# Where the softmax division, the weight loads and a rotary product stand in a hybrid attention layer

## The chip, the cores and the metric

The kernel runs on one core of a Trainium2 chip. Its engines are PE (matrix products), DVE (elementwise and reductions), ACT (activations and copies with a scale), POOL (elementwise, SBUF only) and SP, whose queue issues every DMA of this kernel. The time is device microseconds of one launch, the median of several. All arithmetic is done at about float32 precision: a float32 product is made of three matmuls of split operands (hi x hi, hi x lo, lo x hi), and a probability is carried as two float16 numbers, hi and lo, whose sum it is.

## What is computed

One encoder layer on x (1024 tokens, 1024 features). adaLN gives shift, scale and gate from a conditioning vector. The mixer projects the normalised x and has two groups of heads: 8 heads of multi-head latent attention (MLA; chunk-causal, dense, head size 96 of which 32 are rotary) and 8 heads of chunked attention over a band of 9 chunks of 64 keys with a relative bias (CA; head size 64). Cut to what matters here:

```python
q = jnp.dot(rmsnorm(q_lat, g_q_latent[l]), w_q_up[l]).reshape(B, S, MLA_HEADS, MLA_QK)
kv = jnp.dot(rmsnorm(kv_lat, g_kv_latent[l]), w_kv_up[l]).reshape(B, S, MLA_HEADS, MLA_NOPE + MLA_V)
k_nope, v = kv[..., :MLA_NOPE], kv[..., MLA_NOPE:]
k = jnp.concatenate([k_nope, jnp.broadcast_to(k_rope[:, :, None, :], ...)], axis=-1)
q = rmsnorm(q, g_mla_q[l])
k = rmsnorm(k, g_mla_k[l])
q = jnp.concatenate([q[..., :MLA_NOPE], rope(q[..., MLA_NOPE:], positions)], axis=-1)
k = jnp.concatenate([k[..., :MLA_NOPE], rope(k[..., MLA_NOPE:], positions)], axis=-1)
o_mla = mla_attention(q, k, v)        # softmax(q k^T * scale, masked) v, per head
...
o_ca = chunk_attention(cq, ck, cv, rel_bias[l])
mixed = jnp.dot(jnp.concatenate([o_mla, o_ca], axis=-1), w_out[l])
x = x + g_a[:, None, :] * mixed
h = modulate(rmsnorm(x, g_mlp_norm[l]), sh_m, sc_m)
u = causal_dwconv(jnp.dot(h, w_up[l]), conv_w[l], conv_b[l])
gate, val = jnp.split(u, 2, axis=-1)
x = x + g_m[:, None, :] * jnp.dot(jax.nn.silu(gate) * val, w_down[l])
```

## The kernel before

Tokens come in 8 tiles of 128. The attention is cut into 32 units, a unit being one head and one half (four tiles) of its queries: 16 CA units, then 16 MLA units (lines 814 to 816). A loop over all 128 query tiles (817 to 828) calls `scores` of one tile and `values` of the tile three before. Between them `pace` draws steps from a list of fillers, generators that make the projections: v and q, k of the CA heads, then `m` (the latents), `up0` and `up1` (`f_up`, the up-projections of four MLA heads each) and `oca` (`f_oca`, the CA half of the output projection, kept in DRAM as `part_d`). So the fillers' matmuls run beside the attention of earlier heads. The order of the instructions on each engine is fixed when the kernel is built, by a planner that plays the program through with estimated times and with priorities (`high_priority`); on the chip each engine works its queue in that order and waits at semaphores.

A query tile (`scores`, 636 to 707): PE makes the negated scores into one of two PSUM buffers `S`. DVE adds bias or mask and takes the row minimum m. ACT makes P = exp(m - s) into one of three P buffers, with the row sum. DVE makes the reciprocal of the sum and multiplies it by 2^15 (lines 685, 686). POOL makes hi = float16(P x reciprocal) (`scale_pool`, line 71), DVE makes lo = P x reciprocal - hi (703), both into one of three `hl` buffers, and a DMA transpose on SP's queue (705) brings hi and lo into one of three `PT` buffers. Tiles of more than 640 keys go in two pieces. `values` (709 to 726) multiplies them by v into a PSUM bank; at the end of a unit ACT (723) and DVE (724) take the two halves of v's own split out of it, undo the scales, and a DMA writes the result to `oT_d` in DRAM.

An up-projection (`f_up`, 517 to 582) loads w_q_up's two blocks and w_kv_up's block (526, 532) through `qtile`, a ring of two buffers, splits them (ACT hi, POOL lo), and for each token tile makes q (384 columns) and k, v (512). For q: squares on ACT, their sums on DVE, the reciprocal root on POOL (`rsqrt_mean`, 113 to 116: one instruction scales and adds epsilon, one raises to the power -1/2), the product with it on DVE (561), the rotary turn of 32 of 96 columns on POOL (`rope_apply`, 461 to 470). For k the same, with the rotary part's sum of squares added on POOL (578) and the rotary part, turned earlier in `f_m`, multiplied by the root on POOL (582).

`f_oca` (598 to 611) loads its weights (`load_wo`, 586 to 596, through the same ring) and, for each of 2 x 8 steps, the transposed CA outputs `cl`, splits them, multiplies and stores. After the attention the other half of w_out is loaded (836) and the output projection of the MLA heads runs (873 to 894): `ol` loads the MLA outputs, `pa` the kept part, x1 the residual. Then the MLP's pages, its 22 up-projection steps and the down-projection follow; the change touches nothing there.

Of the kernel before, what the change touches and what calls it, by code (L numbers as in the profile page):

```python
# [41 lines left out]
MODE_C = "1111"  # L42
MODE_M = "1111"
PSCALE, VSCALE = 2.0 ** 15, 2.0 ** 14
# [18 lines left out]
def layer_kernel(ctx, tc, I, out):  # L63
# [273 lines left out]
    def pow2_scale(nm, ssw, b2, n, fac):  # L337
# [13 lines left out]
        dve.tensor_scalar(ab[:, 1:2], t[:, 2, 1:2], 1.0 / (VSCALE * PSCALE), None, op0=MUL)  # L351
# [109 lines left out]
    def rope_apply(o, x, tab, t, nh, tmp):  # L461
# [5 lines left out]
        pool.tensor_tensor(a, x, ct, op=MUL)  # L467
        pool.tensor_tensor(b, x, sn, op=MUL)
        pool.tensor_tensor(o[:, :, 0:16], a[:, :, 0:16], b[:, :, 16:32], op=SUB)
        pool.tensor_tensor(o[:, :, 16:32], a[:, :, 16:32], b[:, :, 0:16], op=ADD)  # L470

    def f_m():
        w = load_w("wm_", I["w_m"], NM)
        lat = {}
        for t in range(NT):
# [17 lines left out]
            lat[t] = raw  # L493
            if j == 3:
# [21 lines left out]

    def f_up(gr):
        if gr == 0:
            right.__exit__(None, None, None)
            for i in "4v3":  # L520
                G["cm" + i] = tc.tile_pool(name="gp" + i, bufs=1, side="right", reuse_waits="tile")
                G[i] = G["cm" + i].__enter__()
        wq = []
        for k in range(2):
            raw = qtile(f"wqr{gr}_{k}")
            sp.dma_start(raw[:, :384], I["w_qu"][gr][:, k, :])
            w = g4([P, 2, 512], F32R, f"wq{gr}_{k}")
            hi_of("a", w[:, 0, :384], raw[:, :384])
            lo_of("p", w[:, 1, :384], raw[:, :384], w[:, 0, :384])
            wq.append(w)  # L530
        raw = qtile(f"wkr{gr}")
        sp.dma_start(raw[:], I["w_kvu"][gr])
# [9 lines left out]
        for t in range(NT):  # L542
            h, j = divmod(t, 4)
            sl = slice(j * P, (j + 1) * P)
            if t % 2 == 0:
# [6 lines left out]
            raw = rtile(f"uqr{gr}_{t}")  # L552
            act.activation(raw[:, :384], pt[:, :384], AF.Copy)
            sq = qtile(f"usq{gr}_{t}")
            act.activation(sq[:, :384], raw[:, :384], AF.Square)
            ss = cst.tile([P, 4], F32, name=f"uss{gr}_{t}", tag="ss", bufs=4)
            r = cst.tile([P, 4], F32, name=f"ur{gr}_{t}", tag="rr", bufs=4)
            dve.tensor_reduce(ss[:], sq[:, :384].rearrange("p (a b) -> p a b", a=4), axis=AX.X, op=ADD)
            rsqrt_mean(r[:], ss[:], QK)
            q_t = mq[gr, t // 2][:, t % 2]  # L560
            dve.tensor_tensor(q_t, raw[:, :384].rearrange("p (a b) -> p a b", a=4),
                              r[:].unsqueeze(2).to_broadcast([P, 4, QK]), op=MUL)
            rope_apply(q_t[:, :, NOPE:], q_t[:, :, NOPE:], tabq, t, 4, raw[:, 0:256])
# [5 lines left out]
            act.activation(r3, p4[:, :, 0:NOPE], AF.Copy)  # L569
            v_t = mv[gr, t // 2][:, t % 2]  # L570
            act.activation(v_t[:, :, 0, :], p4[:, :, NOPE:], AF.Copy, scale=sc)
            dve.scalar_tensor_tensor(v_t[:, :, 1, :], p4[:, :, NOPE:], sc, v_t[:, :, 0, :], op0=MUL, op1=SUB)
            s3 = raw[:, 256:512].rearrange("p (a b) -> p a b", a=4)
            act.activation(s3, r3, AF.Square)
            ss = cst.tile([P, 4], F32, name=f"kss{gr}_{t}", tag="ss", bufs=4)
            r = cst.tile([P, 4], F32, name=f"kr{gr}_{t}", tag="rr", bufs=4)
            dve.tensor_reduce(ss[:], s3, axis=AX.X, op=ADD)
            pool.tensor_tensor(ss[:], ss[:], ssr[:, t:t + 1].to_broadcast([P, 4]), op=ADD)
            rsqrt_mean(r[:], ss[:], QK)
            k_t = mk[gr, t // 2][:, t % 2]  # L580
            dve.tensor_tensor(k_t[:, :, 0:NOPE], r3, r[:].unsqueeze(2).to_broadcast([P, 4, NOPE]), op=MUL)
            pool.tensor_tensor(k_t[:, :, NOPE:], kr[:, t:t + 1, :].to_broadcast([P, 4, ROPE]),
                               r[:].unsqueeze(2).to_broadcast([P, 4, ROPE]), op=MUL)


    def load_wo(k0, n, he, le):
        ws = []
        for k in range(k0, k0 + 4):
            raw = qtile(f"wor{k}_{n}")
            sl = slice(n * 512, (n + 1) * 512)  # L590
            sp.dma_start(raw[:], I["w_out"][k * P:(k + 1) * P, sl])
            w = g4([P, 2, 512], F32R, f"wo{k}_{n}")
# [5 lines left out]
    def f_oca():  # L598
        for n in range(2):
            ws = load_wo(4, n, "a", "p")  # L600
            for t in range(NT):
                lo = rtile(f"cl{t}_{n}", (P, 4, P), F32R)
                hi = rtile(f"ch{t}_{n}", (P, 4, P), F32R)
                sp.dma_start(f32(lo[:]), oT_d[4:8, :, t * P:(t + 1) * P].rearrange("k p t -> p k t"))
                hi_of("a", hi[:], f32(lo[:]))
                lo_of("p", lo[:], f32(lo[:]), hi[:])
                pt = ps.tile([P, 512], F32, name=f"oc{t}_{n}", tag="mm", bufs=2)
                yield from gemm3_f(pt[:], [(hi[:, k], lo[:, k], ws[k][:, 0], ws[k][:, 1]) for k in range(4)])
                o = qtile(f"co{t}_{n}")
                act.activation(o[:], pt[:], AF.Copy)  # L610
# [541 lines left out]
```

## Time and profile before

| | us |
|---|---|
| median of 3 runs | 1465.47 (1463.65 to 1468.99) |
| the profiled execution | 1464.36 |
| its span | 1462.2 |

Busy time over the whole span, and the share of it:

| engine | busy us | share |
|---|---|---|
| PE | 1278.0 | 87% |
| PE's weight loads | 1058.7 | 72% |
| DVE | 1013.6 | 69% |
| ACT | 611.4 | 42% |
| POOL | 823.0 | 56% |

The shares are means over stages with different limits. The stages can be told apart by which instructions run: the start with adaLN and the first projections to about 105 us, the CA units to about 400, the two up-projections to about 510, most of the MLA units to about 660, the output projection and the MLP's first pages to about 780, the up-projection of the MLP to about 1190, the down-projection to the end. A page of the profile gives the span in 40 equal slices; the line of POOL in it, busy tenths, and that of the granted clock of PE, in tenths of full speed:

```profile
POOL 5263554274599954534644555566655555665662
PEclk9979987999787899996887999999999999999998
```

Slices 12 to 14 of POOL (402 to 512 us) stand at 9, 9 and 9, the up-projections. The chain of waits that ended last, followed back through the whole execution, has 39% of the span on PE, 17% on DMA, 15% on DVE, 13% on POOL and 12% in which the engine waited for nothing that the profile shows.

### The profile page before, as it was taken

What the parts mean: (1) busy time and instruction counts of PE and PEld (TensorE: products, weight loads), DVE (VectorE), ACT (ScalarE), POOL (GpSimd) and SP (SyncE); (2) the same over time, 40 slices, a digit from 0 to 9 for tenths busy, and PEclk for the clock granted to TensorE, in tenths of its full rate; (3) what the DMA queues carried; (4) which work ended last, traced back from release to release, by engine and by line L of the source; (5) the groups of instructions that cost most, each with busy time, mean ns of one, the idle gap of its engine ahead of it and who ended that gap; (6) DMA issues with size and microseconds to landing.
All of it is one profiled execution on the core that took longest, in us unless ns stands there. A gap on an engine that the chain in (4) does not pass through costs nothing.

```text
span 1462.2 us, 20198 instructions
## 1 busy us (share of the span) xinstructions
PE 1278.0 (87%) x6836; PEld 1058.7 (72%) x6836; DVE 1013.6 (69%) x1734; ACT 611.4 (42%) x1190; POOL 823.0 (56%) x845
## 2 busy tenths in 40 slices
PE   3859989998967788885776999999999998999997
PEld 2759878886756666664655878788888887887885
DVE  6874776476667868872476887777777777566653
ACT  4453354243455545543274434344444433332331
POOL 5263554274599954534644555566655555665662
PEclk9979987999787899996887999999999999999998
DMA  7323647455522577879611322322222244446442
GB/s 281 134 71 74 131 114 148 129 119 120 112 52 51 115 163 156 180 142 253 246 72 59 105 110 101 116 87 87 87 87 83 75 140 164 151 144 238 146 142 101
DMA packets 218595, 185.94 MB, mean 127 GB/s; under 512 B 148086, under 2 KB 183034, under 8 KB 217468
## 3 DMA queue, kind: packets, MB, share of 16 engines
q1 hardware_dynamic: 218492, 184.66, 44.5%
q8 instruction: 54, 0.88, 0.3%
q14 instruction: 49, 0.40, 0.1%
HBM read 121.17 MB, written 28.84 MB: 103 GB/s over the span
## 4 chain that ended last, share of the span: by engine, by line
PE 39%; DMA 17%; DVE 15%; POOL 13%; issue 12%; ACT 3%; SPq 1%; DVEq 0%; POOLq 0%; ACTq 0%
POOL wds L82 5%; DMA aw<-w_ada 5%; PE p L924 4%; PE p L926 4%; PE p L925 4%; DMA wu<-w_up 3%; DMA PTm<-hlm 3%; PE sc L658 2%; PE dnp L1067 2%; PE dnp L1069 2%; PE dnp L1068 2%; PE sm L658 2%; DVE adacc L243 2%; DVE aacc L430 1%; DVE u L1002 1%
## 5 line engine op out<-in xcount | busy, mean ns | idle before, releaser
L82 POOL TENSOR_TENSOR wds<-wd,wds 128x512 fp32r<-128x512 f32 x88 | 154.6, 1777 | 99.0 <-ACT wds L75 99.0
L82 POOL TENSOR_TENSOR wc<-ws,wc 128x512 fp32r<-128x512 f32 x22 | 65.4, 2972 | 137.8 <-ACT wc L75 137.8
L1057 DVE TENSOR_TENSOR wd<-wd,gmbc 128x1024 f32<-128x1024 f32 x44 | 67.5, 1533 | 80.4 <-DMA wd<-w_down 80.4
L1069 PE MATMUL dnp<-wds,g 128*128 128x512 f32 x308 | 118.4, 390 | 4.5 <-DVE g L82 4.5
L1067 PE MATMUL dnp<-wds,g 128*128 128x512 f32 x308 | 119.6, 390 | 1.9 <-DVE xo L1075 1.9
L75 ACT ACTIVATE wds<-wd 128x512 fp32r<-128x512 f32 x88 | 54.8, 624 | 157.3 <-PE dnp L1069 152.2
L1068 PE MATMUL dnp<-wds,g 128*128 128x512 f32 x308 | 119.5, 389 | 0.0
L71 POOL TENSOR_SCALAR hlm<-Pm,rim 128x512 f16<-128x512 f32 (+4 forms) x88 | 61.9, 706 | 70.1 <-DMA PTm<-hlm 55.1
L703 DVE SCALAR_TENSOR_TENSOR hlm<-Pm,rim,hlm 128x512 f16<-128x512 f32 (+4 forms) x88 | 68.0, 777 | 30.1 <-POOL hlm L71 29.7
L71 POOL TENSOR_SCALAR hlc<-Pc,ric 128x640 f16<-128x640 f32 (+2 forms) x64 | 45.3, 710 | 76.9 <-DVE ric L686 41.2
L1015 DVE TENSOR_TENSOR ws<-wu,wu 128x512 f32<-128x512 f32 x22 | 30.7, 1396 | 76.2 <-DMA wu<-w_up 76.2
L82 DVE TENSOR_TENSOR g<-gr,g 128x512 fp32r<-128x512 f32 x44 | 71.9, 1635 | 11.5 <-ACT g L75 11.5
L1001 DVE SCALAR_TENSOR_TENSOR u<-c,pk,u 128x1023 f32<-128x1023 f32 x44 | 77.4, 1765 | 2.0 <-ACT u L1000 2.0
L1036 ACT ACTIVATE u<-u 128x1024 f32<-128x1024 f32 x22 | 23.4, 1063 | 132.1 <-DVE u L1002 132.1
L683 ACT ACTIVATE Pc<-sc,mc 128x640 f32<-128x640 f32 (+2 forms) x64 | 42.1, 659 | 82.5 <-DVE mc L673 62.0
L658 PE MATMUL sm<-mk,mq 96*128 96x512 f32 (+3 forms) x288 | 68.9, 372 | 7.9 <-ACT Pm L683 7.3
L1000 ACT ACTIVATE u<-c,pk 128x1024 f32<-128x1024 f32 x44 | 52.3, 1236 | 56.2 <-DVE c L1032 56.2
L716 PE MATMUL pvm<-PTm,vt 128*128 128x128 f16 x576 | 50.5, 242 | 28.8 <-DMA PTm<-hlm 24.3
L658 PE MATMUL sc<-k,q 64*128 64x512 f32 (+3 forms) x288 | 70.3, 372 | 4.9 <-ACT Pc L683 3.0
L430 DVE SCALAR_TENSOR_TENSOR aacc<-aw,cs,aacc 128x256 f32<-128x256 f32 x84 | 44.9, 535 | 40.6 <-DMA aw<-w_ada 40.0
L716 PEld LDWEIGHTS <-vt 128*128 128x128 f16 x576 | 41.1, 109 | 41.7 <-issue 38.3
L1069 PEld LDWEIGHTS dnp<-wds,g 128*128 128x128 f32 x308 | 57.8, 188 | 17.7 <-DVE g L82 5.7
(368 smaller groups left out, 4342.0 us busy)
## 6 DMA issues: line engine op xcount, KB each, us to landing
wu<-w_up SPq DMA_DIRECT2D x44, 512.0 KB, 4.3
wd<-w_down SPq DMA_DIRECT2D x44, 512.0 KB, 4.7
aw<-w_ada SPq DMA_DIRECT2D x96, 128.0 KB, 2.3
g_d<-u SPq DMA_DIRECT2D x22, 512.0 KB, 2.6
gr<-g_d SPq DMA_DIRECT2D x44, 256.0 KB, 3.7
x<-x SPq DMA_DIRECT2D x16, 512.0 KB, 8.3
adaw<-w_ada_a SPq DMA_DIRECT2D x8, 1024.0 KB, 5.5
wq_r<-w_qk SPq DMA_DIRECT2D x32, 128.0 KB, 2.6
```

The costliest lines, as they stand in the source:

```text
L71: pool.tensor_scalar(o, i, s, 1.0, op0=MUL, op1=MUL)
L82: (pool if eng == "p" else dve).tensor_tensor(o, i, f32(hi), op=SUB)
L430: dve.scalar_tensor_tensor(acc[:], w[:], cs[:, k:k + 1], acc[:], op0=MUL, op1=ADD)
L658: last = pe.matmul(s[:, c:c + w], qpg[rs_, a, q], kpgs[kh][rs_, b, ko:ko + w], start=(a == 0 and b == 0), stop=(a == 1))
L703: dve.scalar_tensor_tensor(hl[:, w:2 * w], pp, ri[:], hl[:, :w], op0=MUL, op1=SUB)
L716: last = pe.matmul(u.pv[:, c], u.vst(j), mov, start=(x == 0), stop=(x == len(todo) - 1))
L924: pe.matmul(pt, sh, pg[:, 0], start=(k == 0), stop=False)
L1001: dve.scalar_tensor_tensor(u[:, 1:], c[:, :S - 1], pk[:, cv + 1:cv + 2], u[:, 1:], op0=MUL, op1=ADD)
L1057: dve.tensor_tensor(raw[:], raw[:], gmbc[:], op=MUL)
L1067: pe.matmul(pts[t][n], sh, w[n][:, 0], start=(j == 0), stop=False)
L1068: pe.matmul(pts[t][n], sh, w[n][:, 1], start=False, stop=False)
L1069: pe.matmul(pts[t][n], sl, w[n][:, 0], start=False, stop=(j == NF - 1))
```

## The change

Three edits, made together.

1. The exponentials are split undivided. The factor 2^15 goes into the exponent: log(2^15) is added to m on DVE before the exponential. hi is a plain copy of P to float16 on ACT and lo = P - hi on DVE, without a scalar. The sums of a unit's four tiles are kept in one tile; at the end of the unit DVE takes their reciprocals, PE multiplies each, broadcast to 128 columns, by the identity, which lays the reciprocal of every query along the columns of a PSUM bank in all rows, and DVE multiplies the output by it.
2. Loads go one step ahead. `fetch_up` issues the three loads of an up-projection early (for the first at token tile 4 of `f_m`, for the second at token tile 3 of the first); `fetch_wo` does so for blocks of w_out, `split_wo` splits them later, and the MLA half of w_out is loaded and partly split inside `f_oca`. The raw weights stand in the six buffers that the CA heads' v tiles use (`v16`). `f_oca` loads the next step's `cl` before it multiplies the present one.
3. In the up-projection q and k of a token tile share one reciprocal root of eight columns, taken after k's squares are there. The addition of the rotary part's squares (578) and the rotary part's product (582) go from POOL to DVE. `rope_apply` gets an argument for its engine, which stays POOL.

```diff
-PSCALE, VSCALE = 2.0 ** 15, 2.0 ** 14
+LOGP, VSCALE = 15 * math.log(2.0), 2.0 ** 14
...
+            if t == 4:
+                fetch_up(0)
...
+    def vtile(name):
+        return apg.tile([P, 512], F32, name=name, tag="v16", bufs=6)
+
+    def fetch_up(gr):
+        r = up_raw[gr] = [vtile(f"wqr{gr}_{k}") for k in range(3)]
+        for k in range(2):
+            sp.dma_start(r[k][:, :384], I["w_qu"][gr][:, k, :])
+        sp.dma_start(r[2][:], I["w_kvu"][gr])
...
+            if t == 3 and gr == 0:
+                fetch_up(1)
+            if t == 5 and gr == 1:
+                fetch_wo(4, 0)
...
+            ss = cst.tile([P, 8], F32, name=f"uss{gr}_{t}", tag="ss", bufs=4)
+            r = cst.tile([P, 8], F32, name=f"ur{gr}_{t}", tag="rr", bufs=4)
...
-            rsqrt_mean(r[:], ss[:], QK)
-            q_t = mq[gr, t // 2][:, t % 2]
...
+            dve.tensor_reduce(ss[:, 4:8], s3, axis=AX.X, op=ADD)
+            dve.tensor_tensor(ss[:, 4:8], ss[:, 4:8], ssr[:, t:t + 1].to_broadcast([P, 4]), op=ADD)
+            rsqrt_mean(r[:], ss[:], QK)
...
-            pool.tensor_tensor(ss[:], ss[:], ssr[:, t:t + 1].to_broadcast([P, 4]), op=ADD)
-            rsqrt_mean(r[:], ss[:], QK)
...
-            pool.tensor_tensor(k_t[:, :, NOPE:], kr[:, t:t + 1, :].to_broadcast([P, 4, ROPE]),
-                               r[:].unsqueeze(2).to_broadcast([P, 4, ROPE]), op=MUL)
+            dve.tensor_tensor(k_t[:, :, NOPE:], kr[:, t:t + 1, :].to_broadcast([P, 4, ROPE]),
+                              r[:, 4:8].unsqueeze(2).to_broadcast([P, 4, ROPE]), op=MUL)
...
+    def fetch_wo(k0, n):
+        r = wo_raw[k0, n] = [vtile(f"wor{k}_{n}") for k in range(k0, k0 + 4)]
+        for i in range(4):
+            sp.dma_start(r[i][:], I["w_out"][(k0 + i) * P:(k0 + i + 1) * P, n * 512:(n + 1) * 512])
...
     def f_oca():
...
+        lo = fetch(0)
+        for s in range(2 * NT):
+            n, t = divmod(s, NT)
+            hi = rtile(f"ch{t}_{n}", (P, 4, P), F32R)
+            hi_of("a", hi[:], f32(lo[:]))
+            lo_of("p", lo[:], f32(lo[:]), hi[:])
+            nxt = fetch(s + 1) if s + 1 < 2 * NT else None
+            if t == 2:
+                fetch_wo(4 * (1 - n), 1 - n)
...
+            if t == 5:
+                ws.append(split_wo(4 * (1 - n), 1 - n, "a", "p"))
+            lo = nxt
+        fetch_wo(0, 1)
+        wo.append(ws[2])
...
-                act.activation(pr[:, :n], sv, AF.Exp, bias=m[:], scale=-1.0, accum_out=rsum[:, 0:1])
+                dve.tensor_scalar(m[:], m[:], LOGP, None, op0=ADD)
+                act.activation(pr[:, :n], sv, AF.Exp, bias=m[:], scale=-1.0, accum_out=u.rsum[:, i % 4:i % 4 + 1])
             with tc.high_priority(offset=OFF_P):
-                dve.reciprocal(ri[:], rsum[:, 0:1])
-                dve.tensor_scalar(ri[:], ri[:], PSCALE, None, op0=MUL)
...
-                        if mode == "1":
-                            scale_pool(hl[:, :w], pp, ri[:])
...
-                        dve.scalar_tensor_tensor(hl[:, w:2 * w], pp, ri[:], hl[:, :w], op0=MUL, op1=SUB)
+                    act.activation(hl[:, :w], pp, AF.Copy)
+                    dve.tensor_tensor(hl[:, w:2 * w], pp, hl[:, :w], op=SUB)
...
+                    ri = cst.tile([P, 4], F32, name=f"ri{u.nm}_{u.g}", tag="ri", bufs=2)
+                    dve.reciprocal(ri[:], u.rsum[:])
+                    rb = ps.tile([P, 512], F32, name=f"rb{u.nm}_{u.g}", tag="T", bufs=TB)
+                    for j in range(4):
+                        pe.matmul(rb[:, j * P:(j + 1) * P], ri[:, j:j + 1].to_broadcast([P, P]), ident[:],
+                                  start=True, stop=True)
                     act.activation(sb[r0], u.pv[r1], AF.Copy, scale=inv[r1])
                     dve.scalar_tensor_tensor(dst[r0], u.pv[r0], inv[r0], sb[r0], op0=MUL, op1=ADD)
+                    dve.tensor_tensor(dst[r0], dst[r0], rb[r0], op=MUL)
...
-    wo = [load_wo(0, n, "a", "v" if n else "p") for n in range(2)]
+    wo.append(split_wo(0, 1, "a", "v"))
```

More of the change, by code (lines that the diff above doesn't have):

```diff
@@ L598, in f_oca, with fetch @@
     def f_oca():
[L599 to L610, printed above, removed]
-                sp.dma_start(part_d[t][:, n * 512:(n + 1) * 512], o[:])
+        ws = [split_wo(4, 0, "a", "p")]
+        def fetch(s):
+            lo = rtile(f"cl{s}", (P, 4, P), F32R)
+            t = s % NT
+            sp.dma_start(f32(lo[:]), oT_d[4:8, :, t * P:(t + 1) * P].rearrange("k p t -> p k t"))
+            return lo
+        lo = fetch(0)
[7 more added lines that the diff above has]
+                fetch_wo(4 * (1 - n), 1 - n)
+            pt = ps.tile([P, 512], F32, name=f"oc{t}_{n}", tag="mm", bufs=2)
+            yield from gemm3_f(pt[:], [(hi[:, k], lo[:, k], ws[n][k][:, 0], ws[n][k][:, 1]) for k in range(4)])
+            o = qtile(f"co{t}_{n}")
+            act.activation(o[:], pt[:], AF.Copy)
+            sp.dma_start(part_d[t][:, n * 512:(n + 1) * 512], o[:])
+            if t == 5:
[3 more added lines that the diff above has]
+        wo.append(ws[2])
+    wo, wo_raw, up_raw = [], {}, {}
     def qk_page(src, name, rows, tag, bufs, gain):
```

73 lines of the change are left out of this document (26 added, 47 removed).

## The prediction

> **What bounds the kernel now.** I read the busy time by stage first, because the change touches only 105 to 780 us of the span; the 680 us behind that (the gated MLP) and the first 105 us keep their instructions. Columns: PE, PEld, DVE, ACT, POOL busy, granted clock, DMA share, GB/s.
>
> ```profile
> 105.00:200.00 95.00, 94.11 (x751) 85.32 (x749) 59.45 (x176) 38.40 (x90) 41.11 (x53) 1.00 0.45 101
> 200.00:300.00 100.00, 94.36 (x658) 82.60 (x657) 64.44 (x194) 41.09 (x106) 43.11 (x54) 0.85 0.57 130
> 300.00:400.00 100.00, 88.01 (x547) 75.05 (x547) 67.44 (x195) 43.50 (x133) 59.66 (x110) 0.91 0.55 120
> 400.00:440.00 40.00, 26.57 (x122) 20.51 (x122) 28.21 (x79) 21.04 (x55) 37.55 (x74) 0.84 0.26 60
> 440.00:510.00 70.00, 53.69 (x307) 43.48 (x307) 56.05 (x142) 39.41 (x92) 66.88 (x117) 0.81 0.39 81
> 510.00:660.00 150.00, 127.31 (x878) 101.69 (x877) 113.58 (x272) 75.38 (x155) 72.56 (x86) 0.95 0.76 160
> 660.00:780.00 120.00, 74.81 (x342) 58.54 (x341) 66.05 (x82) 50.11 (x85) 54.81 (x49) 0.76 0.54 172
> ```
>
> There are four stages with four limits. The band attention (105 to 400) is bound by PE: its projection matmuls follow one another with some 12 us of gaps after 200. The two up-projections (400 to 510) are bound by POOL (37.55 of 40, 66.88 of 70). The latent attention (510 to 660) has no full engine. What limits it shows in POOL's longest wait of that window (total, times, longest):
>
> ```profile
> POOL hlm L71 <- DMA PTm<-hlm: 50.6, 30, 4.3
> ```
>
> and in the instructions of a probability tile (by shape, whole span: busy, mean ns, idle before):
>
> ```profile
> L703 DVE SCALAR_TENSOR_TENSOR hlm<-Pm,rim,hlm 128x512 f16<-128x512 f32 x40 | 34.1, 853 | 17.3 <-POOL hlm L71 17.2
> ...
> L71 POOL TENSOR_SCALAR hlm<-Pm,rim 128x512 f16<-128x512 f32 x40 | 30.4, 759 | 39.4 <-DMA PTm<-hlm 30.3 <-DVE rim L686 4.2 <-DVE sm L676 2.4
> ...
> L622 DVE TENSOR_TENSOR mq<-mq_ps,mq 96x512 fp32r<-96x512 f32 x16 | 10.8, 677 | 0.1
> ...
> L685 DVE RECIPROCAL rim<-rsm 128x1 f32<-128x1 f32 x64 | 9.7, 153 | 6.2 <-ACT Pm L683 5.8
> ```
>
> POOL stands 50.6 us because the three hl buffers come free only when the DMA transposes of older tiles have landed. The turn of one buffer is hi (0.76), lo (0.85), the landing (3.3, median of the DMA issues) and what each queues for; 64 pieces in 150 us, three at a time, make a turn of 7.0 us. The last stage (660 to 780) begins with weights that come late.
>
> **The rows of the change.** POOL's work in the up-projections (by shape, 400 to 510), and two places where a load is late (ACT's timeline; in brackets the idle time before):
>
> ```profile
> L116 POOL TENSOR_TENSOR kr<-kss,nhalf 128x4 f32<-128x4 f32 x16 | 16.5, 1029 | 0.5
> L116 POOL TENSOR_TENSOR ur<-uss,nhalf 128x4 f32<-128x4 f32 x16 | 16.2, 1010 | 0.2
> ...
> L582 POOL TENSOR_TENSOR kn<-kr,kr 128x128 f32<-128x128 f32 x15 | 8.4, 557 | 0.6
> ...
> L578 POOL TENSOR_TENSOR kss<-kss,ssr 128x4 f32<-128x4 f32 x16 | 4.4, 278 | 0.1
> ```
>
> ```profile
> 444.33 0.42 ACT L535 ACTIVATE wkj<-wkr 128x256 f32<-128x256 f32 x1 [4.94 <-DMA wkr<-w_kvu]
> ...
> 676.34 0.63 ACT L75 ACTIVATE wo<-wor 128x512 fp32r<-128x512 f32 x1 [8.86 <-DMA wor<-w_out]
> ```
>
> **Reciprocals by matmul: a loss in the band stage.** Each of 32 units (16 band, 16 latent) gains four matmuls of 128 columns with an f32 row of reciprocals broadcast as weights. The nearest row is the gate's broadcast, L456: four calls of 256 columns are recorded as 8 matmuls of 377 ns, those of 512 columns take 590, so a call is two passes and a pass costs 213 ns per 256 columns. Four calls of 128 columns are 8 passes of 0.107, 0.86 us, with the change of operands some 0.95 per unit. From below, the transposes of L618 (one pass, four in 0.60 us) give 0.45; from above, 8 weight loads of 0.19 (L456) in the open give 1.5. I take 0.95, because operands and types are those of L456. In the band stage PE has no room: 16 x 0.95 = +15 us (7 to 24). POOL and DVE work that goes there shortens only the 12 or so us that PE stands idle between 200 and 400: -3. Sum +12. In the latent stage 16 x 0.95 falls into 23 us of idle PE, mostly.
>
> **Up-projections: gain.** POOL now does per tile two rsqrts of four columns (1.03 + 1.01, and 0.24 + 0.23 for their scaling), the sum of squares' addition (0.28) and the rotary part (0.56). The eight-column rsqrt is there in the band's norms (L116, 1.65 us; L115, 0.2 to 0.4). So 1.3 to 1.4 us of some 4.6 leave per tile. With the scaling of P (0.7 us, 2 to 4 pieces before 440, 15 after) POOL falls from 37.5 to some 25 in the first window and from 66.9 to 45 in the second. DVE takes up 0.3 for the rotary part (L411, a 128x256 form, is 0.48) and 0.15 for the addition: 8 x 0.45 = 3.6 per window, so 28.2 becomes 32 of 40 and 56.1 some 57. DVE is next: -6 us in the first, -4 in the second. q's rsqrt now waits for k's squares; behind it stand q's rotary products on POOL and q's transposes on PE, and those needed k anyway.
>
> **Loads ahead: gain.** PE ends the first up-projection at 435.6 and starts the second at 445.9; SP issues w_kvu at 441.55 only after POOL's split at 440.5 has freed a buffer, and ACT waits 4.94 us. With the three loads issued at tile 3 (SP needs 0.3 to 0.7 us per issue) only split and scale are left, 2 to 3 us: -8. The first up-projection has the same wait (1.8 us) behind latent transposes that are late themselves: -2. Of the 16 loads of w_out, ACT waits 18.8 us for seven between 660 and 700, and four of them, from 678 to 686, stand in SP's queue ahead of or among the first loads of ol and pa and ahead of all of x. Moved into oca's steps they take 0.5 us each of SP, 8 us of 150, where 64 transposes of 1.23 and some 45 other issues of 0.5 take 102. The first output matmul starts at 682.75; with weights there it can start while the last transposes land. But t = 4 to 7 need the last unit, so I take -7 of the 20 us (0 to -12). Loading cl a step ahead takes ACT's 13.6 us of waiting away, which is off the path.
>
> **Undivided split.** ACT gets hi: 0.63 for 512 columns (L75), 0.52 for 384, so 0.3 to 0.73: 33 us in the band stage, 34 in 510 to 660, where ACT goes from 75 to 110 of 150. DVE loses the two reciprocal steps (0.15 each, L685 and L686), gets the added constant (0.15, in front of the exponential: it delays exp, and behind it PE's scores, by that) and per unit 0.15 + 0.68 (L622) for the final product: per tile -0.30 + 0.15 + 0.21 = +0.06. lo without scalar is a plain subtraction, 0.69 at 512 (L82, DVE on wo), against 0.85: DVE falls from 114 to about 106. A turn of the hl ring becomes 0.13 shorter by hi and 0.16 by lo, and longer by what hi queues behind other work on ACT, where POOL was free for it. Bounds: -20 (a turn 0.9 shorter, 0.9 / 7.0 of 150) and +48 (first rival); nearest to the turn of now I take -3.
>
> The Trainium skill (ScalarE: Activation LUTs, "Rules for kernel authors") speaks against the place of hi: multiplications and additions belong on VectorE, which is faster per element. The rows agree on speed (a scalar product of 1024 columns takes DVE 0.76 at best, L894; ACT's pass of 1024 takes 1.06, L891). By the rule ACT's 64 pieces of the latent stage would cost 0.25 us each too much, 16 us, and the sum would be -2; by the rows ACT has 75 idle us in that stage and DVE 36, and that price is not on the path.
>
> **Sum.** +12 - 2 - 6 - 8 - 4 - 3 - 7 = -18. The profiled execution took 1464.36 (span 1462.2), 1.1 below the median of 1465.47; I predict 1465.5 - 18 = 1447.
>
> **Rivals.** *hi on ACT turns the buffer wait into a wait of the exponentials* (slower). The 50.6 us now stand on POOL, with only splits behind them. On ACT every hi that waits for a landing holds back exp, the Q and K pages and the oca copies. 110 us of work and 50.6 of waiting exceed the stage's 150 by 11; if half of the 75 us that ACT now idles for DVE and PE stays as well, by 48. The middle, +30 in place of my -3, gives 1447 + 33 = 1480. It makes the kernel slower once the stage grows by some 23 us, with ACT's waits for PTm not far under the 50. Against it: exp runs at most three P buffers ahead anyway.
>
> *The ring and the clock both gain.* With fewer gaps PE keeps its clock, which was granted at 0.84 and 0.81 in the up-projections; half-rate time there is 0.32 x 40 + 0.38 x 70 = 39 us. A third of that saved is 13 us at half rate, worth 6, and the ring's -12 on top: 1447 - 18 = 1429. For it: exp to hi needs no other engine now. The Trainium skill (TensorE: Matmul & The Clock Gate, Part 1) says that an idle window of about 3.4 us halves the clock; the low clock in the rows with idle PE agrees.
>
> *The row matmuls cost their upper bound*: +9 in the band stage, +9 in the latent one: 1465, no change.
>
> *The loads do not come early.* The new tiles share six buffers with the values of the band heads, and a load that waits for one holds SP's queue with all transposes behind it. Then -2, -8 and most of -7 go: 1447 + 16 = 1463. Against it: the third buffer needs the third head pair finished, which it is by f_m's fifth tile.
>
> **How the numbers follow.** Forecast 0.44 (its own range 1433 to 1457), ring and clock 0.15, upper-bound matmuls 0.09, loads late 0.06, ACT's wait 0.26. A change under 0.5% (7.3 us) can't be told from none here. Faster 0.59, same 0.15, slower 0.26. The range takes in ring and clock below and most of ACT's case above: 1420 to 1484.
>
> **What would show it.** PE's busy time from 105 to the last band unit up by some 15 us, with 8 matmul records per unit at the new line. POOL under 70% in the up-projections and DVE the fullest. Under 4 us between the two up-projections on PE. No ACT wait for wor behind the last exponential, first output matmul before 678. ACT's wait for PTm under 25 us, and the latent stage no longer than 150. If that wait is 40 us or more, or the stage grows by over 10, the forecast is wrong by the first rival; if the band stage does not grow, PE was not its bound.

## The result, and the profile after

The changed kernel takes 1524.45 us (median of 4 runs, 1522.92 to 1528.99) against 1464.56 before: 1.0415 times, 95% interval 1.0393 to 1.0436. It is slower by 60 us where 18 us less were forecast. Its profiled execution has a span of 1521.1 us, 58.9 more than before.

I cut both executions at the same work, since fixed times no longer meet the same stage: from the first exponential to the first one of unit 15 (the band), from there to the first one of unit 19 (the two up-projections), from there to the last exponential (the rest of the latent attention), and to the end. Windows of before, then of after; columns: length, then PE, PEld, DVE, ACT and POOL busy (instructions), granted clock, DMA share, GB/s.

```profile
106.20:387.60 281.40, 265.40 (x1885) 233.47 (x1884) 181.72 (x536) 114.32 (x312) 136.80 (x208) 0.93 0.52 117
387.60:488.90 101.30, 74.14 (x405) 59.90 (x403) 75.14 (x201) 55.44 (x136) 90.51 (x165) 0.81 0.34 68
488.90:659.60 170.70, 142.92 (x955) 113.80 (x956) 131.60 (x317) 87.47 (x183) 92.98 (x117) 0.93 0.74 157
```

```profile
106.60:400.10 293.50, 272.65 (x1975) 242.76 (x1973) 185.35 (x502) 143.74 (x364) 90.54 (x140) 0.93 0.50 114
400.10:519.60 119.50, 87.87 (x494) 69.04 (x493) 94.02 (x239) 73.85 (x178) 85.36 (x124) 0.84 0.41 96
519.60:735.40 215.80, 168.96 (x1053) 136.37 (x1052) 126.78 (x284) 118.53 (x248) 22.60 (x18) 0.86 0.54 113
```

The band grows by 12, the up-projections by 18, the latent stage by 45; the rest falls by 17 (802.6 to 785.7). In the latent stage PE stands idle for 215.8 - 169.0 = 46.8 us instead of 27.8, although it has more to do, at a clock of 0.86 instead of 0.93. No engine there has a larger share of the stage than before except ACT, and ACT has 97 us free. So something makes the engines wait for each other. The page of the span in 40 slices, POOL and the granted clock, shows POOL nearly empty in slices 15 to 20 (532 to 761 us: the latent stage and the beginning of the rest). That alone is no sign of waiting, since the change itself takes hi away from POOL; in the fastest normalised kernel below it is busy for 29 of 165 us there.

```profile
POOL 5253341242567502000172655666556656665662
PEclk9979989899789889788797899999999999999999
```

The first rival foresaw a slower kernel by ACT's wait for landed transposes. ACT's longest waits in the latent stage after (total, times, longest):

```profile
ACT Pm L710 <- DVE mm L709: 23.6, 15, 4.5
ACT hlm L717 <- DMA PTm<-hlm: 18.2, 19, 2.8
ACT mk L650 <- PE mk_ps L644: 17.5, 9, 5.2
```

The wait for the landing is 18.2 us over 215.8, under the 25 that spoke for the forecast and far from the 40 that spoke for the rival. What is new is the third line: ACT waits 17.5 us for the transposes of k's pages (6.7 in the stage before). The timeline shows why pages are late. Here PE writes the row of reciprocals (`rbm`) of a unit into the bank T:

```profile
604.75 1.11 PE L742 MATMUL rbm<-ident,rim 128*128 128x128 f32 x8
...
611.64 0.61 PE L731 MATMUL pvm<-PTm,vt 128*128 128x128 f16 x8 [0.98 <-DMA PTm<-hlm]
612.28 0.68 ACT L744 ACTIVATE sbm<-pvm,vabm 64x512 f32<-64x512 f32 x1
613.00 0.76 DVE L745 SCALAR_TENSOR_TENSOR om<-pvm,vabm,sbm 64x512 f32<-64x512 f32 x1
...
614.01 0.69 DVE L746 TENSOR_TENSOR om<-om,rbm 64x512 f32<-64x512 f32 x1
...
614.75 1.09 PE L644 MATMUL mq_ps<-ident,qn 128*96 128x128 f32 x4
```

The row is there at 605.9, but it is read only at 614.0, after the unit's last product with v, which waits for the last landing (611.64). T is one bank, and the next q page (`mq_ps`) needs it: it starts as soon as the product has ended, 9 us after the row was there. Over the latent stage a row holds T for about 6 us in the mean and for 8 to 12 in every second unit (first row matmul to the end of the product). Before, q pages were made up to a unit ahead and stood in T themselves (about 8 us in the mean, from a page's first transpose to its last reader); now each waits until the unit two before it has ended, and then stands there for 2.8.

### The profile page after: what moved, and what is told of

It reads as the page before. It is cut to its first block, busy times and chain, and to the rows that moved or that the text cites. A ratio compares the mean times of both kernels' runs of the same rounds, so it can differ in the third digit from the quotient of the medians.

```text
span 1521.1 us, 20527 instructions
## 1 busy us (share of the span) xinstructions
PE 1325.3 (87%) x7092; PEld 1097.7 (72%) x7092; DVE 1032.4 (68%) x1702; ACT 687.1 (45%) x1342; POOL 693.3 (46%) x629
## 4 chain that ended last, share of the span: by engine, by line
PE 54%; DMA 14%; DVE 13%; issue 8%; POOL 7%; ACT 3%; SPq 1%; DVEq 0%; POOLq 0%; ACTq 0%
PE p L945 8%; PE p L947 8%; PE p L946 8%; DMA aw<-w_ada 5%; POOL wds L80 5%; DMA PTm<-hlm 5%; PE sc L684 3%; PE sm L684 2%; PE dnp L1088 2%; PE dnp L1089 2%; PE dnp L1090 2%; DVE adacc L241 1%; PE pvm L731 1%; DVE aacc L428 1%; PE oc L148 1%
## 5 line engine op out<-in xcount | busy, mean ns | idle before, releaser
L1078 DVE TENSOR_TENSOR wd<-wd,gmbc 128x1024 f32<-128x1024 f32 x44 | 71.8, 1633 | 75.9 <-DMA wd<-w_down 74.8
L80 POOL TENSOR_TENSOR cl<-cl,ch 128x512 fp32r<-128x512 f32 x16 | 20.5, 1281 | 158.2 <-ACT ch L73 148.2
L731 PE MATMUL pvm<-PTm,vt 128*128 128x128 f16 x576 | 54.7, 247 | 42.1 <-DMA PTm<-hlm 30.6
L684 PE MATMUL sm<-mk,mq 96*128 96x512 f32 (+3 forms) x288 | 75.7, 389 | 17.9 <-ACT Pm L710 7.7
L718 DVE TENSOR_TENSOR hlm<-Pm,hlm 128x512 f16<-128x512 f32 (+4 forms) x88 | 56.1, 645 | 37.1 <-ACT hlm L717 36.7
L684 PE MATMUL sc<-k,q 64*128 64x256 f32 (+3 forms) x288 | 68.0, 363 | 13.3 <-DVE k L651 6.4
L428 DVE SCALAR_TENSOR_TENSOR aacc<-aw,cs,aacc 128x256 f32<-128x256 f32 x84 | 44.6, 531 | 47.6 <-DMA aw<-w_ada 46.8
L684 PEld LDWEIGHTS sm<-mk,mq 96*128 96x128 f32 x288 | 51.4, 206 | 30.7 <-ACT Pm L710 10.0
L1036 DVE TENSOR_TENSOR ws<-wu,wu 128x512 f32<-128x512 f32 x22 | 24.5, 1115 | 70.0 <-DMA wu<-w_up 70.0
```

Of the source, the lines that this page charges most:

```text
L80: (pool if eng == "p" else dve).tensor_tensor(o, i, f32(hi), op=SUB)
L428: dve.scalar_tensor_tensor(acc[:], w[:], cs[:, k:k + 1], acc[:], op0=MUL, op1=ADD)
L684: last = pe.matmul(s[:, c:c + w], qpg[rs_, a, q], kpgs[kh][rs_, b, ko:ko + w], start=(a == 0 and b == 0), stop=(a == 1))
L731: last = pe.matmul(u.pv[:, c], u.vst(j), mov, start=(x == 0), stop=(x == len(todo) - 1))
L1078: dve.tensor_tensor(raw[:], raw[:], gmbc[:], op=MUL)
```

## The experiments

The order of the instructions on each engine is planned anew for every kernel, so a difference of some us between two of them can be the plan's; where that may decide, the text says so. Below, the stage lengths of each profiled execution, cut as above (band, up-projections, latent, rest), beside the medians and the ratios to the runs of before that were made beside them. The medians of these runs of before lie between 1463.28 and 1469.72, so where a few us between two kernels of different groups decide, the ratios are compared.

| kernel | median us | ratio (95%) | stages us |
|---|---|---|---|
| before | 1464.56 | 1 | 281, 101, 171, 803 |
| the changed kernel | 1524.45 | 1.0415 (1.0393 to 1.0436) | 293, 119, 216, 786 |
| split alone | 1552.23 | 1.0582 (1.0557 to 1.0607) | 300, 116, 228, 799 |
| loads alone | 1479.12 | 1.0089 (1.0063 to 1.0115) | 285, 120, 173, 792 |
| one rsqrt alone | 1465.59 | 0.9982 (0.9964 to 1.0000) | 285, 99, 169, 800 |
| loads and rsqrt | 1471.25 | 1.0023 (1.0011 to 1.0035) | 284, 113, 174, 794 |
| changed, row copied out of T | 1510.74 | 1.0318 (1.0286 to 1.0351) | 302, 116, 192, 786 |
| changed, hi on POOL | 1553.55 | 1.0610 (1.0591 to 1.0629) | 303, 139, 214, 790 |
| changed, no row | 1446.46 | 0.9867 (0.9838 to 0.9895) | 273, 109, 162, 792 |
| loads and rsqrt, splits held | 1464.74 | 1.0010 (0.9997 to 1.0023) | 283, 109, 173, 794 |
| changed, row unused | 1489.77 | 1.0158 (1.0129 to 1.0188) | 284, 116, 189, 791 |
| splits held, divided hi on ACT | 1459.04 | 0.9945 (0.9922 to 0.9969) | 283, 101, 176, 795 |
| before, divided hi on ACT | 1462.50 | 0.9966 (0.9946 to 0.9986) | 276, 105, 169, 805 |
| the same with one rsqrt | 1461.80 | 0.9964 (0.9942 to 0.9986) | 279, 102, 171, 806 |
| changed, row twice, unused | 1538.55 | 1.0479 (1.0437 to 1.0522) | 313, 114, 206, 795 |
| **changed, row in mm** | **1456.27** | **0.9915 (0.9892 to 0.9937)** | 282, 104, 165, 795 |
| changed, row copied, unused | 1505.49 | 1.0250 (1.0208 to 1.0291) | 290, 114, 196, 789 |
| row in mm, splits held | 1468.07 | 1.0009 (0.9988 to 1.0029) | 283, 98, 189, 789 |
| row in mm, no loads | 1484.89 | 1.0123 (1.0100 to 1.0146) | 291, 103, 182, 803 |
| changed, row twice in mm | 1498.60 | 1.0219 (1.0193 to 1.0246) | 308, 103, 187, 790 |

### Which of the three edits

Each edit was put alone on the kernel before, and the split was taken out of the changed kernel; the diffs are the edit's own lines in the diff above, forwards or backwards.

> Only the undivided split, on the kernel before. Theory (the split alone costs: its row of reciprocals holds the single PSUM bank T, or hi queues on ACT; loads and rsqrt gain some 15 to 20 in the last stage): 1525 to 1545 us, above the changed kernel's 1524, since the gain at the end is missing. Rival (the loads or the later q root cost): under 1485.

> Only the loads ahead, on the kernel before. Theory (split costs, loads gain): 1440 to 1457, with the first output matmul less than 10 us behind the last exponential. Rival (loads in SP's queue hold back the transposes, or the values' buffers): 1480 or more.

> Only the one rsqrt and the rotary part on DVE, on the kernel before. Theory (split costs): 1455 to 1468, POOL in the two up-projections 20 us less busy. Rival (q behind k's squares delays the first latent units): 1475 or more.

> The changed kernel with its split undone: loads and rsqrt together. Theory (the split is the whole loss): 1435 to 1455. Rival (loads and rsqrt cost together what neither costs alone): 1490 or more.

The split alone costs 85 us, more than the expected 60 to 80. The loads alone do not gain 8 to 25 us but cost 13, 1 us below the rival's 1480. The one rsqrt gains 0.2%, at the edge of what can be told from nothing. Loads and rsqrt together cost 0.2%, between the two ranges, so inside the changed kernel the split is worth 1524 - 1471 = 53 us of loss. The theory that the split is the whole loss was right for the larger part only; the loads are a second one.

The rsqrt was to relieve the engine that bounded the up-projections. It did relieve it, and nothing followed. The two fixed windows 400 to 440 and 440 to 510 of that run, whose times lie within 4 us of before:

```profile
400.00:440.00 40.00, 28.64 (x142) 22.02 (x140) 33.38 (x89) 23.73 (x58) 30.42 (x45) 0.84 0.31 69
440.00:510.00 70.00, 51.37 (x303) 41.43 (x304) 60.74 (x170) 39.52 (x93) 62.93 (x84) 0.85 0.41 82
```

POOL falls from 37.55 to 30.42 and from 66.88 to 62.93, DVE rises from 28.21 to 33.38 and from 56.05 to 60.74: a relief of 11 us on the one (20 were expected) is a load of 10 on the other, and the stage is 2 us shorter. So POOL at 94% was not all that bound the stage: with POOL at 76% and 90% of the two windows, DVE is at 83% and 87%. That the two, which work for each other tile by tile, now bound it together is argued from these rows and not shown.

### What of the split: hi on ACT, or the row

Three kernels change the changed kernel in one place: the row is copied out of T and the product goes to POOL,

```diff
+                    dve.tensor_copy(dst[r0], rb[r0])
                     act.activation(sb[r0], u.pv[r1], AF.Copy, scale=inv[r1])
-                    dve.scalar_tensor_tensor(dst[r0], u.pv[r0], inv[r0], sb[r0], op0=MUL, op1=ADD)
-                    dve.tensor_tensor(dst[r0], dst[r0], rb[r0], op=MUL)
+                    dve.scalar_tensor_tensor(sb[r0], u.pv[r0], inv[r0], sb[r0], op0=MUL, op1=ADD)
+                    pool.tensor_tensor(dst[r0], dst[r0], sb[r0], op=MUL)
```

hi goes to POOL,

```diff
-                    act.activation(hl[:, :w], pp, AF.Copy)
+                    hi_of("p", hl[:, :w], pp)
```

or the reciprocals, the row and the product go (cut to the main lines).

```diff
-                    dve.reciprocal(ri[:], u.rsum[:])
...
-                        pe.matmul(rb[:, j * P:(j + 1) * P], ri[:, j:j + 1].to_broadcast([P, P]), ident[:],
...
-                    dve.tensor_tensor(dst[r0], dst[r0], rb[r0], op=MUL)
```

A fourth, on the run of loads and rsqrt, queues the splits of the early weights behind an ACT and a POOL instruction of the stage before; it changes the order only.

```diff
+    def behind(k):
+        with tc.issue_after(gate["a", k]), tc.issue_after(gate["p", k]):
+            yield
...
+        with behind(2):
+            ws = [split_wo(4, 0, "a", "p")]
```

> The changed kernel, but the row of reciprocals is copied from PSUM to SBUF by DVE at once, so that the bank T comes free after about 2 us instead of after the unit's last transposed product; the product goes to POOL. PE's and ACT's work stays. Theory T (the row's long hold of T makes the next q page late): 1480 to 1500. Theory A (hi queues on ACT behind copies that wait for PE): 1515 to 1530.

> The changed kernel, but hi is made by POOL (a plain copy to float16), as before the change. Theory A: 1480 to 1500. Theory T: 1512 to 1530, with the row still 9 to 11 us on T in every second latent unit.

> The changed kernel without the reciprocals, their row matmuls and the product with them: the heads' outputs are left unnormalised. Theory T: 1460 to 1480, the latent units back to 13 to 14 us each. Theory A: 1505 or more (only the 32 x 0.95 us of PE and a part of DVE gone).

> Loads ahead and one rsqrt, without the undivided split (1471 in the run before), with the splits of the early weights held in ACT's and POOL's queues: those of the first up-projection behind the last latent tile's squares and rotary turn, the second's behind tile 5 of the first, those of w_out behind tile 5 of the second. Theory H (splits that became ready early were queued ahead of the last latent tiles): 1448 to 1462, latent transposes done some 12 us earlier. Rival (the early loads themselves hold the value buffers or SP's queue): 1467 to 1476.

Without the row the kernel takes 1446, below theory T's 1460 to 1480: the row is worth 78 us, and theory T stands on the place of the loss. Theory A falls, and by its sign: hi back on POOL costs 29 more, which is also above theory T's range. (How it does so stays open; POOL's longest wait in its latent stage is for the exponential, up to 12.6 us, and the plan is another one.) But the copy out of T brought 14 us, not 24 to 44, though the hold of T fell from about 6 to about 3 us in the mean. So the long hold was not all.

Of the splits held: theory H expected 1448 to 1462, the rival 1467 to 1476; 1465 lies between. The latent transposes do end 10 us earlier (406 us instead of 416.5) and the up-projections are 3 us shorter. But what the whole kernel gains is not clear of noise: the medians are 6.5 us apart, the runs of before beside them 4, and the ratios 1.0023 and 1.0010 have intervals that overlap. So the order that H names is there, and its price is small or unknown. POOL's queue in the changed kernel shows the order (start, duration):

```profile
403.81 1.01 POOL L80 TENSOR_TENSOR wq<-wqr,wq 128x384 fp32r<-128x384 f32 x1
404.76 0.24 POOL L467 TENSOR_TENSOR kr<-lat 128x16 f32<-128x16 f32 x1
404.94 0.23 POOL L468 TENSOR_TENSOR kr<-lat 128x16 f32<-128x16 f32 x1
405.12 1.01 POOL L80 TENSOR_TENSOR wq<-wqr,wq 128x384 fp32r<-128x384 f32 x1
406.07 1.28 POOL L80 TENSOR_TENSOR wk<-wqr,wk 128x512 fp32r<-128x512 f32 x1
407.29 1.02 POOL L80 TENSOR_TENSOR wq<-wqr,wq 128x384 fp32r<-128x384 f32 x1
408.40 0.24 POOL L486 TENSOR_SCALAR mss<-mss 128x1 f32<-128x1 f32 x1
...
409.52 0.70 POOL L114 TENSOR_TENSOR mr<-mss,nhalf 128x2 f32<-128x2 f32 x1
410.19 1.00 POOL L80 TENSOR_TENSOR wq<-wqr,wq 128x384 fp32r<-128x384 f32 x1
411.17 0.49 POOL L488 TENSOR_SCALAR lat<-lat,mr 128x256 f32<-128x256 f32 x1
```

The last latent tile's squares, root and scaling (L486, L114, L488) are what the up-projections wait for; between the middle of its rotary part and its scaling stand five weight splits (5.3 us), four of `wq` and one of `wk`, more than one up-projection has: those of the second group are there too. Before the change the raw weights came through a ring of two buffers, so no split could be ready that early. Here the raw weights are there early, the splits are ready early, and the planner queues them early. That an engine works its queue strictly in order is also what the Trainium skill says of ScalarE, VectorE and GpSimd (PSUM — Partial Sum Buffer, "Engine vs sequencer instructions"); the rows agree.

### The row's matmuls, and hi on ACT without a row

The changed kernel without the product that reads the row:

```diff
-                    dve.tensor_tensor(dst[r0], dst[r0], rb[r0], op=MUL)
```

And the divided split of before with hi by ACT, on the held splits, on the kernel before, and on the one rsqrt alone:

```diff
-MODE_C = "1111"
-MODE_M = "1111"
+MODE_C = "0000"
+MODE_M = "0000"
```

> The changed kernel with the reciprocals and their row matmuls on PE, but without the product that reads them: the outputs are left unnormalised, and the bank T is free as soon as the matmuls are done. 1446 without the row, 1524 with all of it. Theory T (the hold and the order it forces are the larger part): 1465 to 1488. Rival (PE's time for the row and its place in PE's queue are the larger part): 1495 to 1520.

> Loads ahead with held splits and one rsqrt (1465), the split divided as before the change, but hi made by ACT with the reciprocal as its scale in place of POOL: no row, no added constant. Theory (hi on ACT is a gain, the row the loss): 1440 to 1455. Rival (the gain of the run without the row was the missing reciprocal ahead of hi): 1460 to 1475.

> The kernel before with one thing moved: hi by ACT with the reciprocal as its scale, in place of POOL. Theory (hi on ACT is a gain): 1440 to 1456. Rival: 1460 to 1475; by the first rival of the prediction (ACT's wait holds back the exponentials) 1480 or more.

> The kernel before with hi on ACT as in the run beside it and with the one rsqrt and the rotary part on DVE, no loads ahead. Theory: 1438 to 1453, some 2 below the run with hi on ACT alone. Rival: as there.

The row's matmuls without their reader cost 43 of the 78 us, 2 us above the range of theory T and below the rival's. Hi on ACT takes the ratio from 1.0010 to 0.9945 on the held splits, from 1 to 0.9966 on the kernel before, and from 0.9982 to 0.9964 (not clear of noise) on the one rsqrt. It never costs, so the prediction's first rival, which would have put the second of them at 1480, is out. But all three are 4 to 9 us above the theory's ranges, and two of them lie in the rival's: of the 25 us between loads with rsqrt (1471) and the run without the row (1446) only a part is hi's place. The rival's cause, the reciprocal in front of hi, is the candidate for the other part; alone it was not tried.

### PE's time, or the bank

On the run with the unused row, every row matmul issued twice:

```diff
+                        for _ in range(2):
```

On the changed kernel, the row in a bank of the fillers:

```diff
-                    rb = ps.tile([P, 512], F32, name=f"rb{u.nm}_{u.g}", tag="T", bufs=TB)
+                    rb = ps.tile([P, 512], F32, name=f"rb{u.nm}_{u.g}", tag="mm", bufs=2)
```

On the run with the copied row, the copy without its reader:

```diff
-                    pool.tensor_tensor(dst[r0], dst[r0], sb[r0], op=MUL)
-                    sp.dma_start(u.dst_d[r0, u.g * 512:(u.g + 1) * 512], dst[r0])
+                    sp.dma_start(u.dst_d[r0, u.g * 512:(u.g + 1) * 512], sb[r0])
```

> The run with the unused row (1490; 44 above the run without it), with every row matmul issued twice. Theory P (those 44 are PE's time, some 1.05 to 2.1 us for each of 32 units, which nothing hides): the same again, 1525 to 1545. Rival (they come from the row's place in the order and its wait, PE's time is mostly hidden): 1493 to 1510.

> The changed kernel with the row in one of the two banks of the fillers (mm) instead of T. Theory T (what the row costs above PE's time, 34, is the hold of T, which makes the next q page late): 1490 to 1510, q pages made up to a unit ahead again. Rival (the product itself and DVE's part at the unit's end): 1518 or more; also if the fillers miss the bank as much as the pages missed T.

> The run in which the row was copied out of T at once (1511), without the product on POOL that reads the copy: the outputs are left unnormalised. Theory (the copy of 0.68 us on DVE and T's 3 us hold are what remains above the unused row's 1490): 1503 to 1514, as with the product. Rival (the product in front of the output's store is on the path): 1488 to 1497.

One word, "mm" in place of "T", turns 1524 into 1456, far past the expected 1490 to 1510. This is the whole change, its output normalised, and it is faster than the kernel before by 0.85% (interval of the ratio 0.9892 to 0.9937). Its three stages, in the order of those above:

```profile
106.90:389.30 282.40, 266.73 (x1994) 237.89 (x1993) 179.45 (x500) 146.54 (x377) 91.30 (x147) 0.97 0.54 118
389.30:492.90 103.60, 76.06 (x419) 60.29 (x418) 90.25 (x232) 69.96 (x163) 77.91 (x111) 0.85 0.43 99
492.90:658.00 165.10, 147.24 (x1083) 120.70 (x1082) 127.27 (x291) 115.82 (x245) 29.05 (x25) 0.99 0.76 155
```

PE has as many row matmuls as in the changed kernel, and they take nearly as long. By shape, changed kernel first:

```profile
L742 PE MATMUL rbc<-ident,ric 128*128 128x128 f32 x128 | 22.4, 327 | 0.0
L742 PE MATMUL rbm<-ident,rim 128*128 128x128 f32 x128 | 20.4, 310 | 2.0 <-DVE modT L447 2.0
```

```profile
L742 PE MATMUL rbm<-ident,rim 128*128 128x128 f32 x128 | 19.4, 297 | 3.3 <-ACT co L629 3.2
L742 PE MATMUL rbc<-ident,ric 128*128 128x128 f32 x128 | 18.7, 287 | 1.5 <-DVE vt L583 1.4
```

42.8 and 38.1 us, of which 40.8 and 36.2 in the three stages. What falls is PE's idle time there, from 99.3 to 61.1 us (length less busy time), and the length of its other work: 529.5 - 40.8 = 488.7 us becomes 490.0 - 36.2 = 453.8. At the clocks of the windows (0.86 to 0.99 in the latent stage, 0.93 to 0.97 in the band) I estimate about 30 of those 35 us as the clock's: in the latent stage (169.0 - 15.2 of row) x (1 - 0.86 / 0.99) = 20, in the band (272.7 - 20.3) x (1 - 0.93 / 0.97) = 10. So by this estimate a good part of what is gained are matmuls at a higher clock, beside the waits that fall away. The Trainium skill gives a rule for this (TensorE: Matmul & The Clock Gate, Part 1: after an idle window of some 3.4 us the array's clock is halved). The runs bear it out only in part: from this kernel to the kernel before and the changed one, the clock of the latent stage falls as PE's idle time grows (0.99 with 17.9 us, 0.93 with 27.8, 0.86 with 46.8), but the run without the loads ahead (below) has 0.90 there with 22.4 us of idle PE and no gap longer than 2.6. So that the stalls are what lowers the clock is not shown here.

What the other bank changes is not how long a row holds it. In mm the rows of the latent stage are held for 10 us in the mean, longer than in T. What it changes is the line of T's users. The q pages stand in T for 6.7 us in the mean again, so they are made ahead; with the row in T but unread it is 3.5, about as short as with all of it, though no row waits there for a reader. Of PE's waits in the latent stage, those for landed transposes fall from 18.4 to 7.1 us and those for the end of the unit before (`om`) from 9.2 to 0.7. So it is shown that the row must not stand among the pages in T; that the length of the hold is what costs is not.

The doubled unused row cost 49 more, as theory P expected. The copied row without its product takes 5 us less than with it (10 by the ratios), in the theory's range: the product is the smaller part of what the copied row costs above the unused one.

### What the repaired kernel still leaves

Three kernels with the row in mm: with the held splits (the two edits shown above, together); without `fetch_up`, `fetch_wo` and the early `cl` (edit 2 backwards); and with every row matmul issued twice, read by the product:

```diff
+                        for _ in range(2):
```

> The whole change with the row in mm (1456) and the early weights' splits held in the queues as in the run of that name. Theory (both repairs add up: holding took 6.5 of 1471): 1446 to 1453. Rival (with the row out of T the early splits harm nothing any more): 1454 to 1458.

> The undivided split with the row in mm and the one rsqrt, without the loads ahead. Theory (loads ahead as the change has them cost 13 alone and 6 beside the one rsqrt): 1443 to 1453. Rival (beside the repaired split the early loads gain in the last stage): 1457 to 1466.

> The whole change with the row in mm and every row matmul issued twice, product included. Doubling the unused row in T cost 49. Theory T (PE's time is mostly hidden, what counts is that T's users stand in one line and the row's time adds to it): 1462 to 1476. Rival P (PE's time for the row is not hidden, in whatever bank): 1490 or more.

All three theories missed, and so did the first two rivals. Doubling the row in mm costs 42, not 6 to 20, as rival P expected: PE's time for a second row is not hidden (in the three stages the doubled row adds 30 us to PE's time and 9 to its idle time). The row's loss in T can be set out by the three stages, which without the row are these:

```profile
108.00:381.40 273.40, 262.37 (x1884) 231.97 (x1883) 168.07 (x471) 145.82 (x378) 93.02 (x147) 0.94 0.55 122
381.40:490.90 109.50, 79.42 (x405) 61.67 (x402) 91.83 (x231) 69.98 (x163) 77.06 (x111) 0.80 0.41 96
490.90:652.80 161.90, 137.48 (x962) 110.71 (x963) 115.57 (x261) 116.93 (x248) 28.44 (x24) 0.97 0.76 156
```

628.8 us with it and 544.8 without: 40.8 are PE's own time for it, 33.8 are idle time (99.3 against 65.5), 9 are other matmuls that take longer; 7 come back in the rest. This sets out where the time stands, not what each part causes: in mm the row takes 36 us of PE as well, and there the first row adds only 10 to the run without a row. Its other matmuls are 26 us shorter than in that run; by the clocks of the windows (0.97, 0.85, 0.99 against 0.94, 0.80, 0.97) I estimate 16 of these as the clock's. Why the clock is higher there, and what of it is the luck of a plan, stays open.

Holding the splits costs 12 beside the repaired row, where without the split it had gained little or nothing. It did shorten the up-projections (98 against 104 us), but the latent stage grew from 165 to 189. PE's idle time in it grew by 14 us (17.9 to 31.6), 6 of them in one place, where the first steps of `oca` stand in PE's queue and wait for `ch`:

```profile
PE oc L148 <- ACT ch L73: 6.2, 2, 4.3
```

And the loads ahead, which cost 13 alone, are worth 29 beside the repaired split: 8 in the last stage (803 against 795), the others in the band (291 against 282) and the latent stage (182 against 165), by a path that stays open. A loss or gain of an edit here holds beside a given plan, and can turn with another edit.

## Why the prediction was wrong

**The step that failed is the row.** "Reciprocals by matmul" was priced as PE's time alone: +12 in the band, nothing in the latent stage ("16 x 0.95 falls into 23 us of idle PE, mostly"). The bank that the row is written to was not in the sum, nor in a rival, though the diff names it (tag "T", one buffer) and the pages' code too. In T the row cost 78 us. In the three stages it took 41 of PE's time (43 in all, 1.34 a unit and not 0.95: 8 records per unit were right, and most units take 1.05 to 1.16 us, but some 2.1 where the granted clock is 0.50) and 34 of idle time. Moved to another bank it cost 10: the term that was left out is T, whose next page has to wait for the row. And PE's idle 23 us in the latent stage did not take it in: idle time that is spread over waits in a chain isn't room for new work on that engine.

**Band, +12 expected, +12 measured, by other parts.** Without the row the band is 273, 8 shorter than before and 11 shorter than with loads and rsqrt alone: the undivided split gains there. With the row, 20 are lost (20.3 of row time on PE). That the band grew as forecast is luck; the run without the row showed what it was made of. The prediction's 12 us of idle PE between 200 and 400 are 17.6 in its own rows (5.6 and 12.0).

**Up-projections, -20 expected (-2, -6, -8, -4), +18 measured.** POOL did fall (85 of 119 us, from 90.5 of 101), and DVE was the fullest. But relieving POOL moved the load to DVE, and with the rsqrt alone the stage is 99 us, only 2 less. The loads alone made 120 of the 101: the splits, ready early, were queued in front of the latents, and holding them back took 3 us of the stage beside the rsqrt (113 to 109); the others stay open. The gap of 10 us between the two on PE did go, as forecast; but one of the same size (412.6 to 422.7) opened inside the first, where the matmuls stand behind the late latent transposes.

**Latent stage, -3 expected, +45 measured.** With the row away the stage is 162, 9 below before, inside the bounds of -20 to +48. The reading of the ring agrees: ACT waits 24.1 us for the landings there, where POOL waited 50.6. The +45 is 54 for the row less these 9.

**Tail, -7 expected, -17 measured for all behind the last exponential.** ACT waits no more for `wor` there, and the first output matmul follows the last exponential by 13 us instead of 23. This term was right in sign and cause. The loads alone make the rest 11 us shorter, against 7; the other 6 come with the row, since without it the rest is 792.

**The rivals.** The first had the sign but not the cause: ACT's wait was under its threshold, and hi on ACT gained where it could be told. The second half of the second, that the clock falls with PE's gaps, has the sign turned: the gaps grew and the clock of the latent stage fell (0.93 to 0.86), though the runs do not show the one as the cause of the other. The third bounded the row by PE's time at 1465 and the run with the row in mm lies at 1456. The fourth, loads that do not come early, is the reverse of what happened: they came too early.

With the row in mm the kernel is where the forecast had put it, 1456 against a range of 1433 to 1457 for the likeliest case, but with other terms: the stages changed by +1, +2, -6 and -8 us, where the sum had +12, -20, -3 and -7. That it comes so near is luck.

## What to carry to other kernels

For every tile that a change adds, ask which buffer it takes, who else takes it, and from when to when it is held: a value must not stand in the line of a single buffer whose next user is the first step of later work. Idle time on an engine is room for new work only if the work fits between the waits. Doubling the suspected operation tells what one more costs (42 us here in mm), which need not be what the first one costs (10). Loads that come early make work ready early, and a queue that is filled by readiness puts it in front of work that is waited for; a ring of few buffers can be what kept the order.

## What was not expected of the hardware

A float32 matmul with 128 columns leaves two records of 0.275 us each that overlap: in the changed kernel a unit's four matmuls take 1.05 to 1.16 us together where the granted clock is 1.00 (604.75 to 605.86 us) and 2.1 where it is 0.50 (305.2 to 307.3). The root of eight columns on POOL takes 1.74 us in the mean there, where before two of four took 1.03 and 1.01, so joining them saves 0.3 us of 2. The granted clock of the latent stage is 0.86 with the row in one PSUM bank and 0.99 with it in another, with nothing else changed but the order that follows from it.
